# A float32 feed-forward and mixer kernel: the norm's product moved behind the fifth step, one sum given from a DMA to VectorE, the first pair's weights through lasting buffers

## The chip, the cores and the metric

The kernel runs on one core of one Trainium2 chip. The metric is the time of one execution on the device in microseconds. Before the change it is 2067.18 us, the median of three runs (2066.85, 2067.18 and 2076.05).

## What is computed

Two layers, each a half feed-forward, a mixer and another half feed-forward, on 512 positions of width 1024:

```python
def swiglu_ffn(x, w_gate, w_up, w_down):
    return (jax.nn.silu(x @ w_gate) * (x @ w_up)) @ w_down
...
for l in range(DEPTH):
    x = x + 0.5 * swiglu_ffn(rms_norm(x, ffn1_norm_w[l]), ffn1_w_gate[l], ffn1_w_up[l], ffn1_w_down[l])
    x = x + hybrid_mixer(rms_norm(x, mix_norm_w[l]), l, w_in[l], w_out[l], ...)
    x = x + 0.5 * swiglu_ffn(rms_norm(x, ffn2_norm_w[l]), ffn2_w_gate[l], ffn2_w_up[l], ffn2_w_down[l])
```

The feed-forward width is 2816. The change touches the feed-forwards alone; the mixer (three kinds of sequence mixing between the products with `w_in` and `w_out`) is the same before and after.

## The kernel before

The program is a list of phases, in this order: feed-forward (0), mixer, feed-forward (1) of the first layer, then the same of the second. The text calls the four feed-forward phases f1(0), f2(0), f1(1), f2(1): half, then layer. The residual stream `x` lies transposed in eight tiles of 128x512 that last through the program.

Every product has float32 accuracy from three products in a shorter format (`mm3`, L114 to L117): high part by high part, high by low, low by high. So each weight block is split when it has landed (`split`, L105 to L112): ScalarE casts the high part `whi` (L110), VectorE subtracts it for the low part `wlo` (L111). Three buffers each hold these parts.

**A pair.** The gate and up products run over 11 pairs of column blocks (`gate_up`). The weights of a pair are a 2x2 block matrix, blocks 11, 12, 21 and 22, each 128x1024 in float32 (512 KB). The 2x2 product is done in seven products in place of eight, the steps of `STEPS` (L196): 11, s1, s2, s4, s3, 12, 22, each 24 TensorE products of 128x256 (four depth slices, two sides, three products). So a pair is 168 of them. Step s1 uses 21+22, s2 uses 11-s1, s4 uses 12+s2, s3 uses 11-21. The seven results are combined in PSUM and in the tile `c`: ScalarE copies the results of 11, s1 and s2 out (`sn`, L339), VectorE adds such a copy to the results of s4 (L341) and 12 (L345), ScalarE copies the results of s3 and 22 into `c` (L343, L347), and a DMA on GpSimd's queue that adds as it writes puts the copy of s1 onto that of s3 (L349). Then `c` is scaled by the norm, twice (L355, VectorE), passed through silu (L356, ScalarE), multiplied (L357) and split into `hh` and `hl` (L360, L361). Step s2 accumulates in the PSUM tile of step 11, so its products wait until ScalarE has copied the result of 11 out.

**Where the weights come from.** `load` (L97 to L104) fills one of four "raw" buffers that last through the whole program; `loadx` (L219 to L224) fills one of six "rx" buffers in a pool of the phase. Both issue on SyncE's queue. Blocks 11, 21, and the two sums go to "rx", blocks 12 and 22 as such to "raw". The sums 21+22 and 12+s2 are formed in flight: the first operand stands in an "rx" buffer, and a DMA on GpSimd's queue adds the second to it (L234, L325). Only pairs 0 and 1 of the first phase form them by VectorE.

**The norm.** The sum of squares of `x` stands in `sqacc`. One product with a matrix of ones (`rms`, L303 to L307; L306, two passes of 128x512) spreads it over the partitions, and 11 VectorE operations (`rstd`, L180 to L185) make the inverse root `rsb` of it. This is called in `after` when pair 0 has issued step 1 of its seven (`n == 1`). The result is first needed when pair 0's `c` is scaled.

**Order.** The Tile framework sorts the instructions of each engine by dependence and priority, so that an instruction's place in the code is not its place in the queue. Loads and splits are given high priority. The down products (`down`) of three finished pairs at a time are woven into later steps by the table `WHEN`; from pair 3 of a phase on there is such work between the steps.

Of the kernel before, what the change touches and what calls it, by code (L numbers as in the profile page):

```python
# [14 lines left out]
ALU = mybir.AluOpType  # L15
# [31 lines left out]
def hybrid_kernel(ctx, tc, aps, phases):  # L47
    nc = tc.nc
    pe, act, dve, pool = nc.tensor, nc.scalar, nc.vector, nc.gpsimd
# [12 lines left out]
    def acc():  # L62
        return acc_pool.tile([P, S], F32, name="acc", tag="acc")

    def aux():
        return aux_pool.tile([P, S], F32, name="aux", tag="aux")

    def side():
        return side_pool.tile([P, S], F32, name="side", tag="side")

    def total():
        return sum_pool.tile([P, S], F32, name="po", tag="po")
# [3 lines left out]
    sqacc = res.tile([P, S], F32, name="sqacc")  # L76
# [16 lines left out]
    ones = const.tile([P, P], F32, name="ones")  # L93
# [5 lines left out]
    def load(src, soon=True):  # L99
        n = src.shape[1]  # L100
        with tc.high_priority() if soon else nullcontext():
            raw = wp.tile([P, WPC], F32, name="raw", tag="raw", bufs=4)
            nc.sync.dma_start(out=raw[:, :n], in_=src)
        return raw  # L104
# [68 lines left out]
    def rstd(ssq, n, vq=None, src=None):  # L173

        shape = list(ssq.shape)
        w = 1
        for m in shape[1:]:
            w *= m
        v, q = vq or (tp.tile(shape, F32, name="rs_v", tag="rs_v%d" % w), tp.tile(shape, F32, name="rs_q", tag="rs_q%d" % w))
        dve.tensor_scalar(v, ssq if src is None else src, 1.0 / n, EPS, ALU.mult, ALU.add)  # L180
        dve.tensor_scalar(ssq.bitcast(I32), v.bitcast(I32), -0.5, float(0x5F3759DF), ALU.mult, ALU.add)
        for _ in range(3):
            dve.tensor_tensor(q, ssq, ssq, ALU.mult)
            dve.scalar_tensor_tensor(q, q, -0.5, v, ALU.mult, ALU.mult)
            dve.scalar_tensor_tensor(ssq, q, 1.5, ssq, ALU.add, ALU.mult)  # L185
# [21 lines left out]
    def ffn(l, which, nxt, first, ctx3):  # L207
# [3 lines left out]
        def cbig(name):  # L211
            return fp.tile([P, 2, 4, 256], F32, name=name, tag="c", bufs=CB)
# [4 lines left out]
        def tmp():  # L217
            return fp.tile([P, S], F32, name="sq", tag="sq", bufs=2)

        def loadx(src, soon=True):  # L220
            with tc.high_priority() if soon else nullcontext():
                raw = fp.tile([P, WPC], F32, name="rx", tag="rx", bufs=RX)
                nc.sync.dma_start(out=raw, in_=src)
            return raw  # L224

        def blocks_of(p):
            w = aps["wgu"][l, which, p]
            soon = not first or p > 1
            r = {"11": loadx(w[0], soon)}
            if soon:  # L230

                r["s1"] = loadx(w[2])
                with tc.high_priority():
                    pool.dma_start(out=r["s1"], in_=w[3], accum_op=ALU.add)  # L234
            return r

        def rest_of(p, r):
            w = aps["wgu"][l, which, p]
            soon = not first or p > 1
            r["21"] = loadx(w[2], soon)  # L240
            if soon:
                r["s4"] = loadx(w[1])
            r["12"] = load(w[1], soon)
            r["22"] = load(w[3], soon)

        def prep_all():

# [39 lines left out]
        if first:  # L287

            with tc.high_priority():
                nc.sync.dma_start(out=pv, in_=aps["pv"])  # L290
                raws0 = {"11": loadx(aps["wgu"][l, which, 0, 0])}
                for d in range(KD):
                    nc.sync.dma_start(out=x[d], in_=aps["xT"][:, d, :])
                nc.sync.dma_start(out=cn, in_=aps["cn"])
                nc.sync.dma_start(out=bc, in_=aps["bc"])
            prep_all()
# [6 lines left out]
        def rms():  # L303

            ps = side()
            pe.matmul(ps, ones, sqacc, start=True, stop=True)  # L306
            rstd(rsb, DM, (tmp(), tmp()), ps)  # L307

        def gate_up(p, after):
            raws = raws0 if first and p == 0 else blocks_of(p)  # L310
            rest_of(p, raws)
            c = cbig("c")
            ps, copies = {}, {}
            for n, (name, f, where) in enumerate(STEPS):
                if name not in raws and name != "s2" and name != "s3":
                    a, b = ("21", "22") if name == "s1" else ("12", "s2")
                    raws[name] = fp.tile([P, WPC], F32, name=name, tag="rx", bufs=RX)
                    dve.tensor_tensor(raws[name], raws[a], raws[b], ALU.add)
                if name in ("s2", "s3"):
                    a, b = (raws["11"], raws["s1"]) if name == "s2" else (raws["11"], raws["21"])  # L320
                    with tc.high_priority():
                        raws[name] = fp.tile([P, WPC], F32, name=name, tag="S", bufs=2)
                        dve.tensor_tensor(raws[name], a, b, ALU.subtract)
                        if name == "s2" and "s4" in raws:
                            pool.dma_start(out=raws["s4"], in_=raws["s2"], accum_op=ALU.add)  # L325
                hi, lw = split(raws[name], 0, 1024)
                if name in ("11", "s1", "s2"):
                    copies[name] = fp.tile([P, 2, 256], F32, name="sn", tag="sn", bufs=4)
                for s in range(2):
                    new = (s, where) not in ps  # L330
                    if new:
                        ps[s, where] = (total() if s and p % 2 else acc()) if where == "X" else aux()
                    out = ps[s, where][:, 0:256]
                    for k in range(4):
                        cc = slice(s * 512 + k * P, s * 512 + (k + 1) * P)
                        r = x_of(f, k)
                        mm3(out, hi[:, cc], lw[:, cc], r[:, 0], r[:, 1], new and k == 0, k == 3, True)
                    if name in copies:
                        act.copy(copies[name][:, s], out)  # L339
                    elif name == "s4":  # L340
                        dve.tensor_tensor(c[:, s, 1], out, copies["s2"][:, s], ALU.add)  # L341
                    elif name == "s3":
                        act.copy(c[:, s, 3], out)  # L343
                    elif name == "12":
                        dve.tensor_tensor(c[:, s, 0], out, copies["11"][:, s], ALU.add)  # L345
                    else:
                        act.copy(c[:, s, 2], out)  # L347
                if name == "s3":
                    pool.dma_start(out=c[:, :, 3], in_=copies["s1"], accum_op=ALU.add)  # L349
                after(n)  # L350
            rb = rsb.rearrange("p (a b) -> p a b", b=256)[:, None].broadcast_to([P, 2, 2, 256])
            g, u = c[:, 0], c[:, 1]
            for t in (g, u):
                t4 = t.rearrange("p (m n) t -> p m n t", m=2)
                dve.tensor_tensor(t4, t4, rb, ALU.mult)  # L355
            act.activation(g, g, AF.Silu)  # L356
            dve.scalar_tensor_tensor(u, g, 0.5, u, ALU.mult, ALU.mult)  # L357
            hh = fp.tile([P, 4, 256], F32R, name="hh", tag="hh", bufs=HB)
            hl = fp.tile([P, 4, 256], F32R, name="hl", tag="hl", bufs=HB)
            act.copy(hh, u)  # L360
            dve.tensor_tensor(hl, u, hh.bitcast(F32), ALU.subtract)  # L361
            hF[p] = [(hh[:, 2 * n:2 * n + 2].rearrange("p a b -> p (a b)"),
                      hl[:, 2 * n:2 * n + 2].rearrange("p a b -> p (a b)")) for n in range(2)]
# [19 lines left out]
        for p in range(KF // 2):  # L383

            when = WHEN[p < 9]
            base = 7 * (p % 3)

            def after(n):
                if p == 0 and n == 1:
                    rms()  # L390
                if first and p == 1 and n == 2:
                    build_bias(lambda name: cbig(name).rearrange("p a b c -> p (a b c)"))
                if first and p in (3, 4, 5, 6) and n == 1:
                    spread_bias(p - 3)
                for _ in range(when.count(base + n)):
                    if todo:
                        down(*todo.pop(0), side())

            gate_up(p, after)
            if p % 3 == 2:  # L400
                todo += [(p // 3, d) for d in range(KD)]
# [747 lines left out]
```

## Time and profile before

| | |
|---|---|
| runs | 2066.85, 2067.18, 2076.05 us; median 2067.18 |
| profiled execution | 2073.17 us |
| its span | 2071.1 us |
| busy | TensorE 95%, VectorE 68%, ScalarE 48%, GpSimd 9% |
| DMA | 309.33 MB; SyncE's queue 231.44 MB, GpSimd's 75.83 MB |

The shares are averages over stages that have different limits. The span is the time between the first and the last instruction of the profiled execution; the time of the execution has 2.1 us around it. The profiled execution is 6.0 us above the median of the runs.

### The profile page before, as it was taken

Reading aid. Unit: us, or ns where it says so; the run is one execution under the profiler, and the core shown is the slowest. Engines: PE = TensorE matmul, PEld = TensorE weight load, DVE = VectorE, ACT = ScalarE, POOL = GpSimd, SP = SyncE. Lnnn points to the kernel's source line nnn. Section 1 sums busy time; section 2 is a strip of 40 time slices with the busy share of each in tenths; the row PEclk is TensorE's granted clock in tenths of the full one; section 3 lists DMA queues with packets and bytes.
Section 4 is the critical chain, followed back from the end, with each engine's and each line's share of the span. In section 5 each row is a group of like instructions: output and inputs, shape, how many; then the busy total and the mean of one; then the engine's idle time right before and its main releaser. Section 6 shows DMA issues by size and latency. Waiting matters only on the chain. (4 is left out here: it accounts for less than half of the span.)

```text
span 2071.1 us, 32422 instructions
## 1 busy us (share of the span) xinstructions
PE 1965.3 (95%) x12766; PEld 1779.7 (86%) x12766; DVE 1418.3 (68%) x2157; ACT 986.0 (48%) x1732; POOL 176.7 (9%) x223
## 2 busy tenths in 40 slices
PE   5899999999998899999968999999999988999999
PEld 4899999889886889999868999989898868899997
DVE  8776675777767666666666776656876685667664
ACT  5544443546544444444444444445475444444442
POOL 0100100020000110000011100000200001100000
PEclk8899999999999899999989999999999989999999
DMA  5766753455413765764376667525544147666633
GB/s 175 207 180 171 191 139 98 136 160 145 128 46 121 191 184 160 191 161 117 106 198 175 186 166 188 139 71 154 174 123 123 41 138 208 180 161 172 185 91 93
DMA packets 113795, 309.33 MB, mean 149 GB/s; under 512 B 11543, under 2 KB 35383, under 8 KB 113644
## 3 DMA queue, kind: packets, MB, share of 16 engines
q1 hardware_dynamic: 82764, 231.44, 34.7%
q0 software_dynamic: 30880, 75.83, 20.2%
q8 instruction: 100, 1.64, 0.3%
q14 instruction: 51, 0.42, 0.1%
HBM read 261.03 MB, written 7.66 MB: 130 GB/s over the span
## 5 line engine op out<-in xcount | busy, mean ns | idle before, releaser
L110 ACT CAST whi<-raw 128x768 fp32r<-128x768 f32 (+3 forms) x288 | 265.0, 920 | 383.4 <-PE side L116 215.3
L111 DVE TENSOR_TENSOR wlo<-raw,whi 128x768 fp32r<-128x768 f32 (+3 forms) x288 | 305.2, 1060 | 108.3 <-ACT whi L110 107.1
L115 PE MATMUL acc<-xT,whi 128*128 128x256 f32 x816 | 237.2, 291 | 29.8 <-ACT sn L339 26.2
L117 PE MATMUL acc<-xT,wlo 128*128 128x256 f32 x816 | 234.6, 288 | 5.0 <-DVE wlo L111 5.0
L116 PE MATMUL acc<-xT,whi 128*128 128x256 f32 x816 | 235.0, 288 | 0.0
L115 PE MATMUL side<-hh,whi 128*128 128x512 f32 x576 | 229.2, 398 | 0.0
L117 PE MATMUL side<-hh,wlo 128*128 128x512 f32 x576 | 226.9, 394 | 0.0
L116 PE MATMUL side<-hl,whi 128*128 128x512 f32 x576 | 225.8, 392 | 0.0
L111 DVE TENSOR_TENSOR wlo<-rx,whi 128x1024 fp32r<-128x1024 f32 x128 | 156.6, 1224 | 94.1 <-ACT whi L110 94.1
L110 ACT CAST whi<-rx 128x1024 fp32r<-128x1024 f32 x128 | 134.1, 1047 | 150.8 <-PE aux L116 87.1
L115 PE MATMUL aux<-xR,whi 128*128 128x256 f32 x704 | 200.5, 285 | 2.0 <-ACT sn L339 1.9
L117 PE MATMUL aux<-xR,wlo 128*128 128x256 f32 x704 | 200.5, 285 | 1.5 <-DVE wlo L111 1.5
L116 PE MATMUL aux<-xR,whi 128*128 128x256 f32 x704 | 200.0, 284 | 0.0
L115 PEld LDWEIGHTS acc<-xT,whi 128*128 128x128 f32 x816 | 160.8, 197 | 35.2 <-ACT sn L339 28.0
L355 DVE TENSOR_TENSOR c<-c,rsb 128x1024 f32<-128x1024 f32 x88 | 107.5, 1221 | 99.9 <-DMA c<-sn 95.9
L117 PEld LDWEIGHTS acc<-xT,wlo 128*128 128x128 f32 x816 | 160.3, 197 | 5.4 <-DVE wlo L111 5.4
L116 PEld LDWEIGHTS acc<-xT,whi 128*128 128x128 f32 x816 | 161.0, 197 | 2.0
L373 DVE TENSOR_TENSOR x<-side,x 128x512 f32<-128x512 f32 x96 | 66.3, 690 | 121.3 <-PE side L117 121.3
L111 DVE TENSOR_TENSOR wlo<-s,whi 128x1024 fp32r<-128x1024 f32 x92 | 112.1, 1222 | 43.1 <-ACT whi L110 43.1
L115 PEld LDWEIGHTS aux<-xR,whi 128*128 128x128 f32 x704 | 136.1, 193 | 3.6 <-ACT sn L339 2.6
L117 PEld LDWEIGHTS aux<-xR,wlo 128*128 128x128 f32 x704 | 135.7, 193 | 2.2 <-DVE wlo L111 2.1
L116 PEld LDWEIGHTS aux<-xR,whi 128*128 128x128 f32 x704 | 136.0, 193 | 1.1
(350 smaller groups left out, 5090.1 us busy)
## 6 DMA issues: line engine op xcount, KB each, us to landing
rx<-wgu SPq DMA_DIRECT2D x172, 512.0 KB, 4.6
raw<-wgu SPq DMA_DIRECT2D x88, 512.0 KB, 4.4
raw<-wd SPq DMA_DIRECT2D x96, 384.0 KB, 3.7
rx<-wgu POOLq DMA_DIRECT2D x42, 512.0 KB, 7.6
rx<-s POOLq DMA_DIRECT2D x42, 512.0 KB, 6.1
raw<-win SPq DMA_DIRECT2D x24, 512.0 KB, 3.8
raw<-winf SPq DMA_DIRECT2D x24, 512.0 KB, 3.6
c<-sn POOLq DMA_DIRECT2D x44, 256.0 KB, 6.2
```

The source lines that it names most:

```text
L110: act.copy(hi[:, :n], raw[:, lo:lo + n])
L111: eng.tensor_tensor(lw[:, :n], raw[:, lo:lo + n], hi[:, :n].bitcast(F32), ALU.subtract)
L115: pe.matmul(out, lh, rh, start=first, stop=False, skip_group_check=skip)
L116: pe.matmul(out, lh, rl, start=False, stop=False, skip_group_check=skip)
L117: pe.matmul(out, ll, rh, start=False, stop=last, skip_group_check=skip)
L355: dve.tensor_tensor(t4, t4, rb, ALU.mult)
L373: dve.tensor_tensor(x[d], ps, x[d], ALU.add)
```

## The change

It has three parts. First, the norm's product is told to keep its place in the program, and `rms()` is called after step index 4 (s3) of pair 0. Second, the sum of the copies of s3 and s1 in `c` is a VectorE operation of 128x2x256 in place of the DMA. Third, `plain(p)` names pairs whose four blocks are loaded as they are through the lasting "raw" buffers, and whose sums are then made by VectorE: pair 0 of every phase, and pair 1 of the first. Behind the change the lines of `gate_up` that stand after the loads have numbers one higher.

```diff
+        def plain(p):
+
+            return p == 0 or first and p == 1
+
         def blocks_of(p):
             w = aps["wgu"][l, which, p]
             soon = not first or p > 1
-            r = {"11": loadx(w[0], soon)}
-            if soon:
-
-                r["s1"] = loadx(w[2])
-                with tc.high_priority():
-                    pool.dma_start(out=r["s1"], in_=w[3], accum_op=ALU.add)
+            if plain(p):
+                return {b: load(w[n], soon) for n, b in ((0, "11"), (2, "21"), (3, "22"), (1, "12"))
+                        if not (first and p == 0 and n == 0)}
+            r = {"11": loadx(w[0]), "s1": loadx(w[2])}
+
+            with tc.high_priority():
+                pool.dma_start(out=r["s1"], in_=w[3], accum_op=ALU.add)
+            r["21"] = loadx(w[2])
+            r["s4"] = loadx(w[1])
+            r["12"] = load(w[1])
+            r["22"] = load(w[3])
             return r
-
-        def rest_of(p, r):
-            w = aps["wgu"][l, which, p]
-            soon = not first or p > 1
-            r["21"] = loadx(w[2], soon)
-            if soon:
-                r["s4"] = loadx(w[1])
-            r["12"] = load(w[1], soon)
-            r["22"] = load(w[3], soon)
...
-                raws0 = {"11": loadx(aps["wgu"][l, which, 0, 0])}
+                raws0 = {"11": load(aps["wgu"][l, which, 0, 0])}
...
         def rms():
 
             ps = side()
-            pe.matmul(ps, ones, sqacc, start=True, stop=True)
+            tc.keep_in_program_order(pe.matmul(ps, ones, sqacc, start=True, stop=True))
             rstd(rsb, DM, (tmp(), tmp()), ps)
...
                 if name == "s3":
-                    pool.dma_start(out=c[:, :, 3], in_=copies["s1"], accum_op=ALU.add)
+                    dve.tensor_tensor(c[:, :, 3], c[:, :, 3], copies["s1"], ALU.add)
...
-                if p == 0 and n == 1:
+                if p == 0 and n == 4:
                     rms()
```

What this moves in the queues is shown at the start of f2(0), where the first layer's mixer ends; f1(1) and f2(1) read alike. In the rows, `xR` and `xT` are the forms of `x` that the seven steps multiply, L115 to L117 are the three products, and a number behind a name tells buffers apart.

TensorE, before: behind the last product with `w_out` (into `aux`) stands the norm's product, and then step 11 of pair 0.

```order
L116 MATMUL aux<-yl_6366,whi 128x512
L117 MATMUL aux<-yh_6365,wlo 128x512
L306 MATMUL side<-sqacc,ones 128x512
L115 MATMUL acc<-xR_6383,whi 128x256
L116 MATMUL acc<-xR_6383,whi 128x256
L115 MATMUL acc<-xR_6383,whi 128x256
```

TensorE, now: step 11 follows the mixer directly, and the norm's product stands behind the last product of s3, ahead of step 12 (into `aux`).

```order
L115 MATMUL acc<-xT,whi 128x256
L116 MATMUL acc<-xT,whi 128x256
L117 MATMUL acc<-xT,wlo 128x256
L306 MATMUL side<-sqacc,ones 128x512
L115 MATMUL aux<-xR_6384,whi 128x256
L116 MATMUL aux<-xR_6384,whi 128x256
```

The norm's product has thus gone behind 120 products of pair 0.

VectorE, before: after the last part of `x` (L171) comes the first half of the norm's chain, and only then the low part of block 11 (L111) and the differences for s2 and s3 (L323).

```order
L171 TENSOR_TENSOR xT<-xt,xT 128x4x256
L180 TENSOR_SCALAR sq<-side 128x512
L181 TENSOR_SCALAR rsb<-sq 128x512
L183 TENSOR_TENSOR sq<-rsb 128x512
L184 SCALAR_TENSOR_TENSOR sq<-sq 128x512
L185 SCALAR_TENSOR_TENSOR rsb<-sq,rsb 128x512
L111 TENSOR_TENSOR wlo<-rx,whi 128x1024
```

VectorE, now: after L171 come the sum for s1 (L319), the differences (L324), and the low parts of s1, s2, s4 and s3 with the sum for s4 among them. The low part of block 11 has gone ahead of these rows, into the end of the mixer.

```order
L171 TENSOR_TENSOR xT<-xt,xT 128x4x256
L319 TENSOR_TENSOR s_6714<-raw 128x1024
L324 TENSOR_TENSOR s_6749<-raw,s_6714 128x1024
L324 TENSOR_TENSOR s_6814<-raw 128x1024
L111 TENSOR_TENSOR wlo<-s_6714,whi 128x1024
L111 TENSOR_TENSOR wlo<-s_6749,whi 128x1024
L319 TENSOR_TENSOR s_6782<-raw,s_6749 128x1024
L111 TENSOR_TENSOR wlo<-s_6782,whi 128x1024
L111 TENSOR_TENSOR wlo<-s_6814,whi 128x1024
```

The same queue goes on with the low parts of blocks 12 and 22, the differences of pair 1 and the low part of its block 11; the new sum (L350) and the norm's chain come behind these.

```order
L111 TENSOR_TENSOR wlo<-raw,whi 128x1024
L342 TENSOR_TENSOR c<-aux,sn 128x256 x2
L111 TENSOR_TENSOR wlo<-raw,whi 128x1024
L324 TENSOR_TENSOR s_7012<-rx 128x1024
L324 TENSOR_TENSOR s_7076<-rx 128x1024
L111 TENSOR_TENSOR wlo<-rx,whi 128x1024
L350 TENSOR_TENSOR c<-c,sn 128x2x256
L180 TENSOR_SCALAR sq<-side 128x512
L346 TENSOR_TENSOR c<-aux,sn 128x256
L181 TENSOR_SCALAR rsb<-sq 128x512
L111 TENSOR_TENSOR wlo<-rx,whi 128x1024
```

The norm's chain has moved from the head of the phase to a place among pair 1's splits.

SyncE's queue, before: behind the last loads of `w_out` come four loads into "raw" (blocks 12 and 22 of pairs 0 and 1) and ten into "rx".

```order
L103 DMA raw<-wout 128x1024 x2
L103 DMA raw<-wgu 128x1024 x4
L223 DMA rx<-wgu 128x1024 x10
L103 DMA raw<-wgu 128x1024
L223 DMA rx<-wgu 128x1024
```

SyncE's queue, now: six loads into the four "raw" buffers, then pair 1's into "rx".

```order
L103 DMA raw<-wout 128x1024 x2
L103 DMA raw<-wgu 128x1024 x6
L223 DMA rx<-wgu 128x1024 x5
L103 DMA raw<-wgu 128x1024
L223 DMA rx<-wgu 128x1024
```

The fifth and sixth "raw" loads are blocks 12 and 22 of pair 1; they need buffers that pair 0 has read, and the five "rx" loads stand behind them.

## Rows read from the trace of the kernel before

**Rows 1.** The profile's page, busy time, share of the span and instructions of each engine.

```profile
PE 1965.3 (95%) x12766; PEld 1779.7 (86%) x12766; DVE 1418.3 (68%) x2157; ACT 986.0 (48%) x1732; POOL 176.7 (9%) x223
```

**Rows 2.** Windows: start:end, length, busy PE, PEld, DVE, ACT, POOL, granted clock, DMA share, GB/s.

```profile
6.80:112.00 105.20, 81.78 (x559) 76.22 (x559) 83.57 (x123) 57.69 (x104) 10.95 (x13) 0.84 0.65 190
660.50:758.30 97.80, 77.97 (x554) 75.15 (x554) 63.76 (x73) 42.60 (x67) 11.52 (x12) 0.87 0.73 194
1039.50:1139.60 100.10, 75.48 (x554) 72.65 (x554) 67.22 (x80) 43.79 (x70) 11.59 (x12) 0.88 0.67 178
1688.10:1785.70 97.60, 76.78 (x555) 73.82 (x554) 63.76 (x73) 42.71 (x67) 11.53 (x12) 0.89 0.73 194
208.00:260.00 52.00, 52.00 (x351) 47.96 (x350) 34.87 (x40) 22.86 (x33) 5.55 (x6) 1.00 0.77 197
```

**Rows 3.** Timeline of TensorE, f2(0): start, length, operation, [idle before <- what ended it].

```profile
664.41 1.73 PE L306 MATMUL side<-sqacc,ones 128*128 128x512 f32 x2 [3.94 <-DVE sqacc L126]
670.69 0.58 PE L117 MATMUL acc<-xR,wlo 128*128 128x256 f32 x1 [3.70 <-DVE wlo L111]
...
671.29 0.41 PE L116 MATMUL acc<-xR,whi 128*128 128x256 f32 x1
671.50 0.41 PE L117 MATMUL acc<-xR,wlo 128*128 128x256 f32 x1
...
682.52 0.28 PE L117 MATMUL acc<-xT,wlo 128*128 128x256 f32 x1
682.64 0.28 PE L115 MATMUL acc<-xT,whi 128*128 128x256 f32 x1
...
700.50 0.28 PE L115 MATMUL acc<-xR,whi 128*128 128x256 f32 x1
...
709.79 0.58 PE L115 MATMUL acc<-xT,whi 128*128 128x256 f32 x1 [3.38 <-ACT sn L339]
...
758.31 0.58 PE L115 MATMUL acc<-xT,whi 128*128 128x256 f32 x1 [4.95 <-ACT sn L339]
```

**Rows 4.** Timeline of VectorE, f2(0).

```profile
664.27 1.22 DVE L171 TENSOR_TENSOR xT<-xt,xT 128x1024 fp32r<-128x1024 f32 x1
...
669.42 1.22 DVE L111 TENSOR_TENSOR wlo<-rx,whi 128x1024 fp32r<-128x1024 f32 x1
...
675.03 2.36 DVE L323 TENSOR_TENSOR s<-rx 128x1024 f32<-128x1024 f32 x2 [1.62 <-DMA rx<-wgu]
...
689.08 1.23 DVE L323 TENSOR_TENSOR s<-rx 128x1024 f32<-128x1024 f32 x1 [1.50 <-DMA rx<-wgu]
...
706.22 1.22 DVE L355 TENSOR_TENSOR c<-c,rsb 128x1024 f32<-128x1024 f32 x1 [6.21 <-DMA c<-sn]
```

**Rows 5.** Timeline of ScalarE, f2(0), between the first and the second pair.

```profile
706.16 1.28 ACT L356 ACT_TABLE_LOAD   x1 [4.27 <-DMA c<-sn]
...
709.38 0.36 ACT L339 COPY sn<-acc 128x256 f32<-128x256 f32 x1
```

**Rows 6.** Timeline of TensorE, starts of f1(0) and f1(1).

```profile
31.12 0.58 PE L115 MATMUL aux<-xT,whi 128*128 128x256 f32 x1 [8.19 <-ACT whi L110]
...
1046.26 2.07 PE L306 MATMUL side<-sqacc,ones 128*128 128x512 f32 x2 [6.80 <-DVE sqacc L126]
```

**Rows 7.** Waits: who <- for whom: us in total, times, longest.

```profile
DVE c L355 <- DMA c<-sn: 95.9, 21, 8.7
```

**Rows 8.** Timeline of GpSimd, f2(0): the sum 21+22 of pair 1.

```profile
677.56 1.21 POOL L234 DMA_DIRECT2D rx<-wgu  x1
```

**Rows 9.** The page's DMA issues: what, queue, count, KB each, median us to landing.

```profile
rx<-wgu SPq DMA_DIRECT2D x172, 512.0 KB, 4.6
...
rx<-wgu POOLq DMA_DIRECT2D x42, 512.0 KB, 7.6
...
c<-sn POOLq DMA_DIRECT2D x44, 256.0 KB, 6.2
```

**Rows 10.** VectorE's groups by form: busy us, mean ns of one.

```profile
L126 DVE TENSOR_TENSOR sqacc<-sqacc,sq 128x512 f32<-128x512 f32 x42 | 28.8, 686 | 0.6
```

More of the change, by code (lines that the diff above doesn't have):

```diff
@@ L305, in rms @@
             ps = side()
-            pe.matmul(ps, ones, sqacc, start=True, stop=True)
+            tc.keep_in_program_order(pe.matmul(ps, ones, sqacc, start=True, stop=True))
             rstd(rsb, DM, (tmp(), tmp()), ps)
         def gate_up(p, after):
-            raws = raws0 if first and p == 0 else blocks_of(p)
-            rest_of(p, raws)
+            raws = blocks_of(p)
+            if first and p == 0:
+                raws["11"] = raws0["11"]
             c = cbig("c")
```

## The prediction

> **What bounds the kernel now.** The page comes first: TensorE is busy 95% of the span [rows 1], so it is the bound on the whole, and at most 5% could be had from filling its idle time. That is an average, so I looked next for the stretches in which it isn't full, with windows [rows 2]. In a steady stretch of a feed-forward (the last row) TensorE is busy 52.00 of 52.00 us at a granted clock of 1.00: nothing done for another engine can shorten such a stretch. The first four rows are the starts of the four feed-forward phases, from the first product of pair 0 to the first of step s2 of pair 3. Each holds three pairs of 168 products, 48 more of pair 3, and the norm's product: 552 of the 128x256 products. One such product follows the last after 0.12 us at full clock (682.52 to 682.64) and after 0.21 us at the lower level (671.29 to 671.50) [rows 3]. At full clock 552 take 66.2 us; the four stretches took 105.2, 97.8, 100.1 and 97.6 us at clocks of 0.84 to 0.89 [rows 2]. About 136 us lie there: partly waits, partly the lower clock that follows each of them.
>
> The timeline of f2(0) shows where. TensorE ends the mixer at about 660.5 and waits 3.94 us for `sqacc`, since the norm's product stands ahead of step 11. Step 11 then does what it can with high parts and waits 3.70 us for its low part [rows 3]: VectorE has run half the norm's chain between L171 (664.27) and that split (669.42) [rows 4]. Then the differences wait for sums in flight (675.03, and 689.08 for pair 1) [rows 4]. Pair 1 begins at 700.50 [rows 3], 40 us after pair 0, whose 168 products need 20.2.
>
> A second loss is at the pair boundaries. At 709.79 and 758.31 TensorE waits 3.38 and 4.95 us for ScalarE's copy of step 11 [rows 3]. The copy (709.38) is queued behind silu, whose table load starts at 706.16 [rows 5], and VectorE's scaling of `c`, begun at 706.22, had waited for the DMA that puts s1 onto s3 [rows 4]. That DMA is the last to come for `c` 21 times, 95.9 us in all, 8.7 at the longest [rows 7]; these are VectorE's waits, and most of them cost TensorE nothing.
>
> **Part one, the norm's product behind s3, with part three, pair 0's blocks as they are.** I walk f2(0) anew. Step 11 needs neither the norm nor the last part of `x`, and its split now stands in the mixer's tail: 660.5 + 24 x 0.12 = 663.4. Steps s1 and s2 need L171, which ends at 665.5 [rows 4]. Behind it stand the sum, two differences and the split of s1: four operations at a spacing of 1.14 us (two take 2.36, one 1.22 [rows 4]), so s1 can start at 670.0, and the split of s2 follows in time. From there: s1 and s2, 48 x 0.12 = 5.8; about 20 products at the lower clock after the wait (an estimate; the products at 671.29 and 671.50 stand in such a stretch), 20 x 0.094 = 1.9 more; s4 and s3, 5.8; the norm, 1.7 [rows 3]; 12 and 22, 5.8. Pair 0 ends at 691.0, where before it was 700.50: **9.5 us**. The two sums added on VectorE (2.4 us) are in this walk; the two loads and two adding DMAs that go are queue work that TensorE didn't wait for in other pairs, and I give them nothing.
>
> What hides the rest of the norm's chain: `rsb` is first needed at the end of pair 0. Its 11 operations, at most 0.69 us each by the same shape [rows 10], have the whole of pair 1 to run in, 20 us, with silu of pair 0 behind them; pair 1's products don't need them. If that cover fails, silu again stands ahead of a copy on ScalarE.
>
> The moved loads. On SyncE's queue blocks 12 and 22 of pair 1 now wait for two of the four lasting buffers, and the five "rx" loads stand behind them. The buffers are free once s3's difference has read them, at about 668.9. The first operand of pair 1's sum lands 4.6 us later [rows 9], 673.5; the sum in flight took 11.5 us here before (677.56 [rows 8] to the end of VectorE's wait at 689.08 [rows 4]), its median is 7.6 [rows 9]. By the longer one it lands at 685.0, and two differences and a split make 688.5. Pair 1 is due at 691.0: a margin of 2.5 us, so I give it no cost.
>
> **Part two, the sum by VectorE.** It adds 44 operations of 512 elements per partition, 0.69 us by the nearest shape [rows 10], 30 us on an engine that idles 32%. It removes 44 DMAs of 6.2 us median [rows 9] from the path of `c`. The sum follows ScalarE's second copy of s3 at once, and steps 12 and 22 (5.8 us) still lie ahead, so scaling no longer waits for it. Pairs 1, 2 and the first 48 products of pair 3 then take 384 x 0.12 = 46.1 us: 691.0 + 46.1 = 737.1 against 758.31, **21.2 us** in f2(0), 9.5 of it from parts one and three.
>
> The Trainium skill, "DMA: Bandwidth & Descriptors", section "Anatomy of one DMA — SWDGE (gpsimd) path", gives such a DMA 2.0 us and its bytes over 436e3, an estimate of 2.6 us for these 256 KB. By it the waits of 3.38 and 4.95 us would be mostly something else's, and part two would bring about 1 us a phase.
>
> **The other phases.** The walk makes f2(0) 76.6 us long (660.5 to 737.1). f2(1) has the same mixer tail: 97.6 - 76.6 = 21.0. In f1(1) the last `sqacc` came 2.9 us later (6.80 us of waiting against 3.94 [rows 3, 6]), which stays: 100.1 - 79.5 = 20.6. f1(0) had its sums on VectorE already, and VectorE's preparation of `x` holds it (8.19 us of waiting at 31.12 [rows 6]; VectorE is busy 83.57 of 105.2 [rows 2]). There only boundary waits can go, between nothing and 105.2 - 83.6 - 2.1 = 19.5; I take two like those of f2(0), 8.
>
> Sum: 21.2 + 20.6 + 21.0 + 8 = 70.8 us. Something is given back: VectorE would be busy 63.8 + 2.4 + 3 x 0.69 = 68.3 of 76.6 us in f2(0), so small waits will come in pairs 1 and 2. I allow each one recovery at the lower clock: 2 x 4 x 1.9 = 15 us. That leaves **56 us**. The profiled execution would go from 2073.2 to about 2017; it stands 6.0 above the median, so the median goes from 2067.2 to **2011**.
>
> **The rivals.**
> - *Pair 1 comes late.* Seven loads set free at one moment crowd each other, and SyncE's queue holds them all until 668.9. For it: 1.50 us of waiting at 689.08 with loads less delayed [rows 4]. Against it: the margin of 2.5 us. Fully late, pair 1 starts where it started before and 9.5 us a phase are lost, three times: 56 - 28 leaves 28, **2039**.
> - *The removed DMA was not what was late.* Another wait takes its place at the boundary, such as the sum in flight for the next pair or scaling behind other VectorE work. Then only pair 0 is shorter: 3 x 9.5 = 28, again **2039**. For it: the next load in rank is as slow, 7.6 us [rows 9]. Against it: ScalarE's table load, VectorE's scaling and TensorE's wait follow each other within 4 us of that DMA's landing [rows 3 to 5]. By its page on DMA, named above, the Trainium skill would have it this way; the median of 6.2 us here is over twice that estimate. If both rivals hold, nothing is left: **2067**.
> - *VectorE's queue is held by the new sum (slower).* The sum waits at the head of VectorE's queue for s3's second half (12 x 0.12 = 1.4 us) and ScalarE's copy (0.36 [rows 5]), then takes 0.69: 2.5 us in which no split runs. If TensorE needs the split behind it at once, each of 44 pairs pays: 110 - 56, **2121**. It decides from 1.3 us a pair, where it eats the gain. Against it: at pair 0 the splits of 12, 22 and of pair 1's 11 stand ahead of the sum in the order, so that TensorE has 5.8 us of work in hand.
> - *Nothing is given back.* No recovery in pairs 1 and 2, and f1(0) gains up to its bound: 70.8 + 11.5, about **1985**.
>
> **How the numbers follow.** My forecast has 0.52, nothing given back 0.10, pair 1 late 0.15, another wait at the boundary 0.12, both 0.06, a held VectorE 0.05. About 10 us, 0.5%, is what a measurement of this kernel can tell from no change. The first four lie beyond that on the fast side: faster 0.89, same 0.06, slower 0.05. The range goes from 1986 to 2045: it holds the forecast and the two rivals at 2039 with 6 us to spare, and leaves out most of the last rival above and the two worst cases.
>
> **What would show it.** Right: at the start of f2(0) step 11 follows the mixer without a wait; step s1 starts near 670 and pair 1 near 691; the windows to step s2 of pair 3 take 77 to 81 us at a clock over 0.9; no wait of scaling for a DMA is left; TensorE's waits for the copy of step 11 are gone at the first boundaries. Wrong: pair 1 starts at 695 or later with VectorE's difference waiting for a sum in flight (first rival); TensorE still waits for the copy at the second and third boundary (second); new TensorE waits for splits in the steady stretches, their busy share under 52 of 52 (third).

## The result and the profile after

The changed kernel takes 2017.39 us (median of four runs, 2011.88 to 2018.65), against 2071.21 for the kernel before in the same comparison: a ratio of 0.9734 with a 95% interval of 0.9701 to 0.9768. Forecast were 2011, between 1986 and 2045. The profiled execution went from 2073.17 to 2018.65 us, 54.5 less, where 56 were forecast. The total was right; the terms it was made of were not all right, and some errors cancelled. The changed kernel's executions fall into two groups, near 2011 and near 2018 us, in this comparison and in its repetition ("Once more", median 2011.43); what decides between them was not found, and both profiled executions belong to the upper group.

The page after, its first part (answers to [rows 1]) and the line of GpSimd's DMA queue, which moved 75.83 MB before:

```profile
PE 1941.6 (96%) x12766; PEld 1761.9 (87%) x12766; DVE 1446.8 (72%) x2207; ACT 991.9 (49%) x1732; POOL 117.5 (6%) x173
...
q0 software_dynamic: 18048, 61.15, 15.7%
```

The same four stretches as in [rows 2], from the first product of pair 0 to step s2 of pair 3, and a steady one; columns as there:

```profile
7.00:111.00 104.00, 81.55 (x558) 77.11 (x559) 89.04 (x128) 59.72 (x106) 7.64 (x11) 0.87 0.59 183
659.10:741.10 82.00, 71.59 (x556) 69.46 (x555) 68.29 (x80) 43.61 (x68) 6.60 (x8) 0.96 0.70 203
1019.60:1107.70 88.10, 73.77 (x555) 71.39 (x554) 73.38 (x91) 45.22 (x73) 6.59 (x8) 0.90 0.66 189
1651.30:1733.90 82.60, 71.96 (x555) 69.63 (x555) 68.22 (x79) 43.58 (x68) 6.55 (x8) 0.96 0.69 201
763.90:989.90 226.00, 226.00 (x1531) 209.05 (x1531) 150.55 (x164) 102.86 (x152) 9.60 (x11) 1.00 0.50 140
```

Before they were 105.2, 97.8, 100.1 and 97.6 us long. The clock in f2(0) and f2(1) rose from 0.87 and 0.89 to 0.96, and the steady stretch is full, as it was. VectorE's busy time in f2(0) is 68.29 us; 68.3 were worked out.

TensorE's timeline of f2(0) answers to [rows 3]:

```profile
659.10 0.28 PE L115 MATMUL acc<-xR,whi 128*128 128x256 f32 x1
...
666.55 0.58 PE L115 MATMUL aux<-xT,whi 128*128 128x256 f32 x1 [4.42 <-ACT whi L110]
...
687.87 0.28 PE L115 MATMUL acc<-xR,whi 128*128 128x256 f32 x1
...
689.66 0.39 PE L117 MATMUL acc<-xR,wlo 128*128 128x256 f32 x1 [1.39 <-DVE wlo L111]
...
701.69 0.39 PE L117 MATMUL aux<-xR,wlo 128*128 128x256 f32 x1 [3.01 <-DVE wlo L111]
...
713.83 0.39 PE L117 MATMUL acc<-xR,wlo 128*128 128x256 f32 x1 [1.50 <-DVE wlo L111]
...
741.05 0.28 PE L115 MATMUL acc<-xT,whi 128*128 128x256 f32 x1
```

Step 11 follows the mixer at once (659.10), and pair 1 begins at 687.87, 28.8 us later; before it was 40. Step s1 starts with ScalarE's cast of its sum (`whi`), before VectorE has split it. The waits for ScalarE's copy of step 11 are gone, here and in the whole execution; before, TensorE's waits had this line (us in total, times, longest):

```profile
PE acc L115 <- ACT sn L339: 26.2, 9, 4.9
```

Three new waits for VectorE's low parts stand in pairs 1 and 2: 1.39, 3.01 and 1.50 us. VectorE's timeline there, and the queues of SyncE and GpSimd, say where these come from (answers to [rows 4, 8]):

```profile
686.11 2.36 DVE L324 TENSOR_TENSOR s<-rx 128x1024 f32<-128x1024 f32 x2 [5.33 <-DMA rx<-wgu]
688.38 1.22 DVE L111 TENSOR_TENSOR wlo<-rx,whi 128x1024 fp32r<-128x1024 f32 x1
689.52 0.68 DVE L350 TENSOR_TENSOR c<-c,sn 128x512 f32<-128x512 f32 x1
...
699.28 1.23 DVE L324 TENSOR_TENSOR s<-rx 128x1024 f32<-128x1024 f32 x1 [3.40 <-DMA rx<-wgu]
...
710.29 2.36 DVE L356 TENSOR_TENSOR c<-c,rsb 128x1024 f32<-128x1024 f32 x2
712.56 1.22 DVE L111 TENSOR_TENSOR wlo<-rx,whi 128x1024 fp32r<-128x1024 f32 x1
```

```profile
630.52 38.17 SPq L103 DMA_DIRECT2D raw<-wgu  x6
668.85 2.42 SPq L223 DMA_DIRECT2D rx<-wgu  x2
```

```profile
677.63 0.86 POOL L239 DMA_DIRECT2D rx<-wgu  x1 [72.60 <-DMA rx<-wgu]
```

SyncE holds pair 1's "rx" loads until 668.85, behind the six "raw" ones; GpSimd starts pair 1's sum in flight at 677.63, when its first operand has landed; VectorE waits until 686.11 for it, with the split of pair 1's block 11 (688.38) next in its queue, and TensorE waits for that. At 699.28 the same happens with pair 2's sum, and a split for pair 1 stands behind it. The third wait has another cause: from 699.28 on VectorE works without a pause, and the split of pair 2's block 11 (712.56) stands behind the rest of the norm's chain and the scaling of pair 0 (710.29).

### The profile page after: what moved, and what is told of

It reads as the page before. It is cut to its first block, busy times and chain, and to the rows that moved or that the text cites. A ratio compares the mean times of both kernels' runs of the same rounds, so it can differ in the third digit from the quotient of the medians.

```text
span 2016.5 us, 32318 instructions
## 1 busy us (share of the span) xinstructions
PE 1941.6 (96%) x12766; PEld 1761.9 (87%) x12766; DVE 1446.8 (72%) x2207; ACT 991.9 (49%) x1732; POOL 117.5 (6%) x173
## 5 line engine op out<-in xcount | busy, mean ns | idle before, releaser
L110 ACT CAST whi<-raw 128x1024 fp32r<-128x1024 f32 (+3 forms) x293 | 269.8, 921 | 443.2 <-PE side L116 221.5
L111 DVE TENSOR_TENSOR wlo<-raw,whi 128x1024 fp32r<-128x1024 f32 (+3 forms) x293 | 311.4, 1063 | 119.7 <-ACT whi L110 118.6
L115 PE MATMUL acc<-xT,whi 128*128 128x256 f32 x816 | 232.8, 285 | 0.8 <-ACT c L344 0.5
L116 PE MATMUL acc<-xT,whi 128*128 128x256 f32 x816 | 231.8, 284 | 0.0
L117 PE MATMUL acc<-xT,wlo 128*128 128x256 f32 x816 | 230.9, 284 | 0.1
L115 PE MATMUL side<-hh,whi 128*128 128x512 f32 x576 | 229.2, 398 | 0.0
L117 PE MATMUL side<-hh,wlo 128*128 128x512 f32 x576 | 226.9, 394 | 0.0
L117 PE MATMUL aux<-xR,wlo 128*128 128x256 f32 x704 | 201.3, 286 | 9.9 <-DVE wlo L111 9.9
L115 PE MATMUL aux<-xR,whi 128*128 128x256 f32 x704 | 203.0, 288 | 7.1 <-ACT whi L110 7.1
L110 ACT CAST whi<-rx 128x1024 fp32r<-128x1024 f32 x117 | 122.6, 1048 | 140.1 <-PE aux L116 71.3
L111 DVE TENSOR_TENSOR wlo<-rx,whi 128x1024 fp32r<-128x1024 f32 x117 | 143.1, 1223 | 61.4 <-ACT whi L110 61.4
L115 PEld LDWEIGHTS acc<-xT,whi 128*128 128x128 f32 x816 | 157.8, 193 | 4.8 <-ACT c L344 1.6
L111 DVE TENSOR_TENSOR wlo<-s,whi 128x1024 fp32r<-128x1024 f32 x98 | 119.4, 1223 | 58.4 <-ACT whi L110 58.1
L116 PEld LDWEIGHTS acc<-xT,whi 128*128 128x128 f32 x816 | 157.7, 193 | 2.0
L117 PEld LDWEIGHTS acc<-xT,wlo 128*128 128x128 f32 x816 | 156.6, 192 | 0.5 <-DVE wlo L111 0.5
L117 PEld LDWEIGHTS aux<-xR,wlo 128*128 128x128 f32 x704 | 136.7, 194 | 10.6 <-DVE wlo L111 10.6
L115 PEld LDWEIGHTS aux<-xR,whi 128*128 128x128 f32 x704 | 137.0, 195 | 9.9 <-ACT whi L110 7.3
L110 ACT CAST whi<-s 128x1024 fp32r<-128x1024 f32 x98 | 102.5, 1048 | 76.5 <-PE acc L116 26.7
```

Of the source, the lines that this page charges most:

```text
L110: act.copy(hi[:, :n], raw[:, lo:lo + n])
L111: eng.tensor_tensor(lw[:, :n], raw[:, lo:lo + n], hi[:, :n].bitcast(F32), ALU.subtract)
L115: pe.matmul(out, lh, rh, start=first, stop=False, skip_group_check=skip)
L116: pe.matmul(out, lh, rl, start=False, stop=False, skip_group_check=skip)
L117: pe.matmul(out, ll, rh, start=False, stop=last, skip_group_check=skip)
```

## The experiments

Twelve runs were made: eleven further kernels, and the changed kernel once more. Each ratio is to the kernel before as it ran in the same comparison (medians 2069.59 to 2071.67). The table gives, for f2(0), how long after the mixer's last product pair 1 starts, and how long pairs 1 to 3 then take until pair 4 starts (both from TensorE's timeline, us). Full, the second is 68.85.

| kernel | median us | ratio to before, 95% interval | pair 1 starts | pairs 1 to 3 |
|---|---|---|---|---|
| before | 2071.21 | 1 | 40.2 | 83.1 |
| changed | 2017.39 | 0.9734 (0.9701 to 0.9768) | 28.8 | 76.0 |
| part two alone | 2028.79 | 0.9791 (0.9767 to 0.9815) | 38.3 | 68.9 |
| part one alone | 2045.36 | 0.987 (0.9831 to 0.9909) | 40.4 | 76.4 |
| part three alone | 2049.05 | 0.9891 (0.9866 to 0.9917) | 28.4 | 81.3 |
| one and three | 2042.48 | 0.9856 (0.983 to 0.9883) | 28.7 | 82.9 |
| one and two | 2016.60 | 0.974 (0.9725 to 0.9754) | 39.5 | 68.9 |
| two and three | 2014.43 | 0.973 (0.9714 to 0.9747) | 28.7 | 77.1 |
| changed, two loads on GpSimd's queue | 2005.31 | 0.9686 (0.9672 to 0.9701) | 28.9 | 70.8 |
| changed, pair 1 plain too | 2010.63 | 0.9714 (0.9696 to 0.9732) | 29.1 | 75.1 |
| two loads on GpSimd's queue, no pin in f1(0) | **1993.58** | 0.9631 (0.96 to 0.9663) | 29.1 | 70.4 |
| two loads on GpSimd's queue, no pin | 2004.28 | 0.9682 (0.9657 to 0.9708) | 28.8 | 74.5 |
| changed, a second operation like the sum | 2022.26 | 0.9769 (0.9744 to 0.9794) | 27.7 | 77.5 |
| changed, once more | 2011.43 | 0.9719 (0.9694 to 0.9744) | 28.8 | 73.1 |

The windows of that second stretch in five of them (before, part two alone, part three alone, changed, changed with two loads on GpSimd's queue), one fence each:

```profile
700.50:783.57 83.07, 74.75 (x542) 72.57 (x541) 53.54 (x56) 38.78 (x60) 8.92 (x9) 0.92 0.69 186
```

```profile
697.49:766.35 68.86, 68.86 (x543) 67.25 (x542) 54.83 (x59) 39.50 (x60) 5.20 (x6) 1.00 0.74 212
```

```profile
685.98:767.32 81.34, 72.70 (x542) 69.68 (x541) 56.49 (x63) 38.61 (x60) 9.84 (x11) 0.96 0.76 200
```

```profile
687.87:763.83 75.96, 70.00 (x543) 67.51 (x542) 64.95 (x76) 39.35 (x60) 6.99 (x8) 1.00 0.73 201
```

```profile
689.07:759.86 70.79, 69.35 (x543) 67.33 (x541) 59.79 (x68) 39.61 (x60) 5.20 (x6) 1.00 0.73 204
```

With part two alone TensorE is busy 68.86 of 68.86 us at clock 1.00. With part three alone pair 1 starts as early as in the changed kernel, but pairs 1 to 3 stay long. In f2(0) TensorE waits 4.41 us for a split behind pair 2's sum and 2.53 for ScalarE's copy of step 11, and 13.5 us of gain are left at pair 4; in f2(1) pairs 1 to 3 take 93.8 us, and 0.7 is left.

**Part two alone.**

```diff
-                    pool.dma_start(out=c[:, :, 3], in_=copies["s1"], accum_op=ALU.add)
+                    dve.tensor_tensor(c[:, :, 3], c[:, :, 3], copies["s1"], ALU.add)
```

> The kernel before with part two alone: the sum of s3's and s1's copies by VectorE. Theory (the DMA was the last to come for c, and scaling, silu and ScalarE's copy stood behind it): TensorE's waits for the copy of step 11 at the pair boundaries (3.4 and 5.0 us in f2(0)) go with the lower clock after them, 7 to 12 us in each of three phases, so 21 to 36 under the kernel before. Rival (another wait takes the DMA's place): within 8 us of the kernel before. Rival (the sum holds VectorE's queue): slower than before.

Measured: 42 us under the kernel before, more than either bound. No wait of TensorE for the copy of step 11 over 1 us is left in f2(0), and pairs 1 to 3 are full. That the DMA was the last to come is shown, and the first rival falls for the three later phases. In f1(0) it holds: to pair 4 that phase is only 1.4 us shorter (128.05 before, 126.66), since VectorE there waits 7.59 us for pair 2's sum in flight where it waited 7.57 for this DMA, and TensorE 4.26 behind it where it waited 5.04. The Trainium skill's "DMA: Bandwidth & Descriptors", section "Anatomy of one DMA — SWDGE (gpsimd) path", gives an estimate of 2.6 us for such a DMA of 256 KB. The trace disagrees with a median of 6.2 us [rows 9], and so does the gain of 42 us, where by that estimate almost nothing was to be had; the measurement decides.

**Part one alone, part three alone, one and three.** The first has these lines (numbers of the kernel before); the second has `plain(p)` and the loads of the diff above and neither other part; the third has all but part two.

```diff
-            pe.matmul(ps, ones, sqacc, start=True, stop=True)
+            tc.keep_in_program_order(pe.matmul(ps, ones, sqacc, start=True, stop=True))
...
-                if p == 0 and n == 1:
+                if p == 0 and n == 4:
```

> The kernel before with part one alone: the norm's product pinned behind s3. Theory (parts one and three need each other, since pair 0's s1 waits for its sum in flight, which landed at 675.0 in f2(0), as well as for the norm's chain): pair 0 ends 1 to 5 us earlier in each of three phases, so 3 to 15 under the kernel before. Rival (the norm's chain alone was what held pair 0): the whole 11 us a phase, 30 to 36 under it.

> The kernel before with part three alone: pair 0's blocks through the lasting buffers and its sums by VectorE, the norm's product where the scheduler puts it. Theory (the norm's chain still stands ahead of pair 0's operations on VectorE, 4 us of it before the first split): 3 to 20 under the kernel before. Rival (the sums in flight alone held pair 0): 30 to 36 under it. Rival (the loads moved behind two buffers of pair 0 make pair 1 late, and nothing is won): within 5 us of the kernel before.

> The changed kernel with part two undone, so parts one and three together. Theory: pair 0 ends 11 us earlier in each of f2(0) and f2(1) and some less in f1(1), the boundary waits stay: 25 to 35 under the kernel before, so 20 to 30 over the changed kernel. Rival (the boundary waits came from pair 0's late start and go with it): within 8 us of the changed kernel.

Part one alone won 26 us, which neither theory had. In f2(0) pair 0 ends no earlier (pair 1 starts at 40.4, before at 40.2, where 1 to 5 us less were expected), and the gain is at another place. With the norm's chain late, scaling of pair 0 comes when the DMA has long landed. VectorE's timeline of that kernel, where [rows 4] has a wait of 6.21 us for the DMA:

```profile
707.20 0.68 DVE L185 SCALAR_TENSOR_TENSOR rsb<-sq,rsb 128x512 f32<-128x512 f32 x1
...
710.07 2.35 DVE L355 TENSOR_TENSOR c<-c,rsb 128x1024 f32<-128x1024 f32 x2
```

So it cures the first pair boundary too, by another way than part two. Part three alone won 22 us, just over what its theory had, and moved pair 1 to 28.4 by itself: it was the sum in flight, not the norm's chain, that held pair 0 in f2(0). In f1(1) pair 1 starts 6.8 us earlier with part one alone and 10.8 with part three alone, so there the chain had a share too. One and three together won 29 us (25 to 35 expected). The single gains, 42, 26 and 22, make 90; together they are 54.

**One and two, two and three.** The changed kernel with part three undone, and with part one undone.

> The changed kernel with part three undone (pair 0's sums in flight again, its loads where they were), so parts one and two. Theory (what part three gains in pair 0, 11 us a phase, pairs 1 and 2 give back, since their loads stand behind two buffers that pair 0 reads): 0 to 12 over the changed kernel, about 2017 to 2029. Rival (part three's gain is kept): 28 to 35 over the changed kernel.

> The changed kernel with part one undone (the norm's product where the scheduler puts it), so parts two and three. Theory (with part three the split of pair 0's steps no longer waits for the norm's chain wherever the product stands, as pair 1 began 28 us into the phase with part three alone too): within 6 of the changed kernel. Rival (the chain at the head of VectorE's queue costs its 7.4 us in each of three phases): 15 to 25 over the changed kernel.

Both equal the changed kernel within the intervals of the totals. By phases, counted to the start of pair 4 (TensorE's timeline), they differ. The three later phases together take 369.6 us before, 326.8 with part two alone, 323.8 with one and two, 323.6 with two and three, and 321.0 in the changed kernel; f1(0) takes 128.1, 126.7, 121.1, 117.2 and 126.8. So in the later phases the other two parts bring some 3 us each once part two is there. In f1(0) the pin of part one takes back 9.6 us of what parts two and three win. Part three's 11 us at pair 1 of f2(0) are in the main given back: without it pairs 1 to 3 are full (68.9), with it they take 76.0.

**Two loads on GpSimd's queue.**

```diff
-    def load(src, soon=True):
+    def load(src, soon=True, queue=None):
...
-            nc.sync.dma_start(out=raw[:, :n], in_=src)
+            (queue or nc.sync).dma_start(out=raw[:, :n], in_=src)
...
-            r["12"] = load(w[1])
-            r["22"] = load(w[3])
+            r["12"] = load(w[1], queue=pool if p == 1 else None)
+            r["22"] = load(w[3], queue=pool if p == 1 else None)
```

> The changed kernel with blocks 12 and 22 of pair 1 issued on GpSimd's queue, so that pair 1's five other loads no longer stand behind two buffers on SyncE's queue. Theory (this hold, until 668.9 in my sum and 668.85 in the changed kernel's trace, makes pair 1's and pair 2's sums in flight late): those loads go 6 to 9 us earlier, pairs 1 and 2 lose 0 to 3 us a phase in place of 7, and the kernel is 8 to 20 under the changed kernel, about 1997 to 2009. Rival (VectorE, busy nearly throughout these pairs, or the rate of the DMA engines gives it back): within 5 of the changed kernel.

Measured 2005.31, 12 under the changed kernel, within the theory, and 6 under its repetition. The stretches say more than the medians: the three later phases take 301.9 us to pair 4, where the two profiled executions of the changed kernel took 321.0 and 316.8. Its queues (SyncE, GpSimd) and VectorE in f2(0):

```profile
660.15 10.24 SPq L223 DMA_DIRECT2D rx<-wgu  x5
```

```profile
669.53 1.25 POOL L103 DMA_DIRECT2D raw<-wgu  x2 [63.74 <-DVE s L324]
670.77 0.91 POOL L239 DMA_DIRECT2D rx<-wgu  x1
```

```profile
681.89 2.35 DVE L324 TENSOR_TENSOR s<-rx 128x1024 f32<-128x1024 f32 x2
```

The phase starts at 660.20 here and at 659.10 in the changed kernel. Counted from there, the "rx" loads go at once in place of 9.8 us later, the sum in flight is issued after 10.6 us in place of 18.5, and VectorE's difference no longer waits. Pairs 1 to 3 take 70.8 us. That the hold on SyncE's queue was the cause of pair 1's lateness is thereby shown; VectorE's load or the DMA rate would have given it back. The third wait of the changed kernel stays (1.23 us at 709.42, behind the scaling of pair 0): that one is VectorE's load.

**Pair 1 plain too.** `plain(p)` returns `p < 2`.

> The changed kernel with pair 1 of every phase loaded as it is too, with no sum in flight for it. Theory (the hold on SyncE's queue is what costs, and four loads now wait for pair 0's buffers): 0 to 15 over the changed kernel. Rival (the sums in flight are what makes pair 1 late): 5 to 15 under it.

2010.63 is 7 under the first median of the changed kernel (2017.39) and 1 under the second (2011.43), within both intervals: nothing can be told from it.

**The pin taken from f1(0), and from all phases**, both on the kernel with the two loads moved.

```diff
-            tc.keep_in_program_order(pe.matmul(ps, ones, sqacc, start=True, stop=True))
+            mm = pe.matmul(ps, ones, sqacc, start=True, stop=True)
+            if not first:
+                tc.keep_in_program_order(mm)
...
-                if p == 0 and n == 4:
+                if p == 0 and n == (1 if first else 4):
```

> The last but one kernel (pair 1's two blocks on GpSimd's queue) with the norm's product pinned in three phases alone; in the first phase it stands where it stood before, called behind step 1. Theory (in the first phase the pin pushes the norm's chain behind pair 1's splits on VectorE, and with it the scaling of pair 0 and the copies of the bias, for which TensorE waits 5 us at 80.4 in the changed kernel): f1(0) 8 to 10 us shorter, the kernel at 1994 to 1999. Rival (f1(0) is held by VectorE's preparation of x, and gives it back): 2003 to 2007.

> The same with the norm's product pinned nowhere. Theory (the pin is worth nothing in the later phases either once part three is there): within 3 of the kernel that pins it in three phases. Rival (the chain ahead of pair 1's splits shows once the loads are no longer late): 4 to 20 over it.

Without the pin in f1(0) the kernel takes 1993.58 us, the fastest of all, 12 under the one with the pin everywhere. The stretch of f1(0) to pair 4 in the changed kernel and in this one:

```profile
7.05:133.87 126.82, 104.42 (x715) 98.36 (x715) 104.25 (x146) 69.31 (x120) 9.02 (x12) 0.89 0.61 186
```

```profile
6.92:124.36 117.44, 100.50 (x714) 94.91 (x715) 103.31 (x146) 68.52 (x120) 9.04 (x12) 0.91 0.66 202
```

And what the pin does there, in the changed kernel, on VectorE and on TensorE:

```profile
71.28 0.68 DVE L185 SCALAR_TENSOR_TENSOR rsb<-sq,rsb 128x512 f32<-128x512 f32 x1
72.00 2.36 DVE L356 TENSOR_TENSOR c<-c,rsb 128x1024 f32<-128x1024 f32 x2
...
78.64 1.23 DVE L362 TENSOR_TENSOR hl<-c,hh 128x1024 fp32r<-128x1024 f32 x1
79.90 0.48 DVE L427 COPY brow<-side 4x320 f32<-4x320 f32 x1
```

```profile
80.44 1.22 PE L426 MATMUL side<-oh,rb 33*4 33x320 f32 x2 [4.87 <-DVE brow L427]
```

The chain ends at 71.28, and the copy of the bias (L427) stands in VectorE's queue behind all that waits for it; the bias products share one PSUM tile (`side`), so the second of them stops TensorE until the first is copied. In the kernel without the pin in f1(0) that copy comes at 66.40, and this wait is gone. Without any pin the kernel loses the 11 us again in the later phases (2004.28; pairs 1 to 3 take 74.5 us): my theory that the pin is worth nothing there fell. It is worth little only as long as the loads are late.

**A second operation like the sum.**

```diff
+                    dve.tensor_tensor(copies["s1"], copies["s1"], copies["s1"], ALU.max)
                     dve.tensor_tensor(c[:, :, 3], c[:, :, 3], copies["s1"], ALU.add)
```

> The changed kernel with a further VectorE operation of the same size and place as the new sum, 44 times (the larger of the copy of s1 and itself, which changes nothing). Theory (the new sum's 0.69 us lie beside TensorE's work in the steady pairs and cost little at the phase starts): 0 to 6 over the changed kernel. Rival (VectorE's queue is held by the sum): 44 x 0.69 = 30 over it.

4.9 over the changed kernel by the medians and 10.8 over its repetition; 30 are excluded. To pair 4 the four phases take 445.7 us together, where the two profiled executions of the changed kernel took 447.8 and 443.3: the sum lies beside other work, and VectorE's queue is not held by it.

**Once more.**

> The changed kernel once more, unchanged. The second layer's mixer took 294.7 us in its profiled execution and 299.2 in the kernel before, with the same instructions. Theory (that difference, all of it at one wait, varies from execution to execution and is no part of the change): it may come at 299 us here, with the feed-forward phases within 1 us of what they were, and the kernel at 2014 to 2021. Rival (the change shortens the mixer): 294 to 296 us again.

2011.43 (2010.83 to 2018.32): the median is below what was expected. The second layer's mixer, before, in the changed kernel, and in this run of it:

```profile
1388.73:1688.10 299.37, 296.35 (x1764) 253.65 (x1762) 219.49 (x519) 158.97 (x351) 22.96 (x41) 0.98 0.42 119
```

```profile
1356.66:1651.36 294.70, 291.42 (x1765) 250.59 (x1764) 220.56 (x520) 159.83 (x352) 23.02 (x41) 1.00 0.43 119
```

```profile
1349.97:1648.60 298.63, 296.15 (x1764) 254.05 (x1763) 220.65 (x520) 160.25 (x352) 22.95 (x41) 0.98 0.42 117
```

So the mixer's 4.7 us were not the change's. They are not one wait either, as I had written: TensorE is idle 3.0, 3.3 and 2.5 us in the three, and its busy time differs, with the granted clock (0.98, 1.00, 0.98). That the feed-forward phases would repeat within 1 us was wrong: pairs 1 to 3 took 73.1 us here in place of 76.0, so their waits differ from execution to execution.

## Why the prediction was right, and where it was not

- **What bounds the kernel** held: full steady stretches, and all of the gain but the mixer's 4.7 us in the starts of the phases.
- **Part one with part three, 9.5 us a phase at pair 1.** Measured in f2(0): 40.2 to 28.8, 11.4. But I had put it on both parts; in f2(0) part three alone does it, part one alone does not. The walk began with the right rows (VectorE's sum right behind L171), but let s1 wait for VectorE's two differences and its split too; s1 starts with ScalarE's cast of the sum, at 666.55, 7.4 us into the phase, where I had 9.5. So the walk ended 1.7 us too late (30.5 us into the phase, measured 28.8).
- **The margin of 2.5 us for pair 1** is the step that failed in f2(0). Counted from the phase's start (660.5 in my walk, 659.1 in the run), the hold on SyncE's queue ended after 9.8 us where I had 8.4. For the sum's first operand I took the median of all loads, 4.6 us; GpSimd could start only 8.8 us after the hold, since the loads set free together land later (7.7 us by the median between 666 and 682). The sum itself then took less than the 11.5 us I gave it, and was there after 27.0 where I had 24.5. With pair 0 ending after 28.8 in place of 30.5 the margin became a wait, and pair 2's sum made a second one. The first rival, to which I gave 0.15, is in part what happened: 7.1 us of the 11.4 are given back in f2(0), and "one and two" comes to the same total without part three. I had also taken it that the norm's chain and the scaling of pair 0 would run beside pair 1 at no cost; the third wait (1.50 us) stands behind them.
- **Part two, 21.2 - 9.5 = 11.7 us a phase** by full pairs behind pair 0. Pairs 1 to 3 went from 83.1 to 76.0, and to 68.9 with part two and no part three. The mechanism and its full size are as written; the changed kernel does not reach it. The 3.8 us a phase taken off for recoveries covered about half of the 7.1 given back in f2(0).
- **The other phases.** f1(0) was to gain 8 us and gained 1.2 (128.05 to 126.82 at pair 4), since the pin moved the bias copies; this was not in my sum at all. The 8 were carried over from f2(0)'s waits for the copy of step 11, which f1(0) didn't have; it had one of 5.04 us for a split behind the same DMA. Without the pin, parts two and three win 10.8 us there. In f1(1) the stretch to s2 of pair 3 went from 100.1 to 88.1, 12 us, for 20.6 less the allowance: VectorE and ScalarE prepare `x` there while the last down products run, and s1 starts 12.0 us into the phase, where I had carried over f2(0)'s start and 2.9 us.
- **The total.** My terms were for the stretches to s2 of pair 3: less the allowance 17.4 us in f2(0), 17.2 in f2(1), 16.8 in f1(1) and 4.2 in f1(0), 55.6 together. There the gains are 15.8, 15.0, 12.0 and 1.2, 44.0 together, 11.6 less. Most of the difference was made up by two things outside the sum. Between s2 of pair 3 and pair 4, f2(0) and f2(1) each need 22.8 us where they needed 25.3, since the third boundary wait is gone and with it the lower clock behind it; that is 5 us. And the second layer's mixer happened to be 4.7 us shorter. So the mechanism held, but that 54.5 us came out in the profiled executions where 56 were forecast is in part luck.
- **The signs.** Of those written down beforehand, the windows to s2 of pair 3 in the three later phases missed: 82.0, 88.1 and 82.6 us, for 77 to 81, and in f1(1) the clock was 0.90, not over it. Pair 1 started early enough, with VectorE's difference waiting for a sum in flight none the less.
- **The rivals.** Slower by a held VectorE: excluded, nobody waited for the sum, and its 0.684 us were as estimated (0.69). The removed DMA not late, or another wait in its place: excluded by part two alone in the later phases; in f1(0) it is what happened there. Nothing given back: not this kernel, but two further edits came near its 1985 us, with 1993.58.

## What to carry to other kernels

Gains at one place are not summed from parts that cure the same wait: here three parts of 42, 26 and 22 us alone make 54 together, and the second with either of the others makes as much. When loads go through a small set of lasting buffers, look at what stands behind them on the issuing queue, since a load that waits for a buffer holds every load behind it, and time the loads that are then set free by the crowded ones. A pin that helps in three phases can cost in a fourth that has other work in the same queue: check each place where the line runs.

## What was not expected of the hardware

When pair 0 had read its buffers, seven loads of 512 KB were set free together (668 to 672 us), and they crowded each other: in a window from 666 to 682 us SyncE's "rx" loads took 7.7 us to landing by the median, where it is 4.7 over the whole execution of the changed kernel, and the DMA engines were busy nearly throughout from 669 to 678 us. The changed kernel's DMA view of that window has this line (loads, KB each, median us to landing):

```profile
rx<-wgu SPq DMA_DIRECT2D x6, 512.0 KB, 7.7
```

The first operand of pair 1's sum came 8.8 us after the hold, so that the sum waited longer for it than the sum itself took (8.5 us, from GpSimd's issue at 677.63 to the end of VectorE's wait at 686.11).
